# Instance norm over 512 channels: from 32 units of 4 MB in six slots to 23 units of 4 or 6 MB in four slots

## The chip, the cores and the metric

One Trainium2 chip, one of its cores. A core has TensorE (PE), VectorE (DVE), ScalarE (ACT), GpSimd (POOL) and SyncE (SP), a local memory of 128 partitions, a small accumulation memory that TensorE writes (PSUM), and 16 DMA engines that carry data between the chip's main memory and the local one. The metric is the device time of one execution in microseconds (us), lower is better. The kernel before takes 626.87 us (median of 3 runs, 626.81 to 627.3).

## What is computed

```python
def setup_inputs():
    B, G, C_per_g, H, W = 4, 8, 16, 256, 256
    return {
        "x": np.random.randn(B, G, C_per_g, H, W).astype(np.float32),
        "gamma": np.random.randn(G, C_per_g).astype(np.float32),
    }

def reference(x, gamma):
    mu = x.mean(axis=(3, 4), keepdims=True)
    var = ((x - mu) ** 2).mean(axis=(3, 4), keepdims=True)
    x_norm = (x - mu) / np.sqrt(var + 1e-5)
    return (x_norm * gamma[None, :, :, None, None]).astype(np.float32)
```

There are 4 x 8 x 16 = 512 channels of 65,536 float32 values each, 134.2 MB in and 134.2 MB out. Each channel gets its own mean and variance, and one of 128 gammas. A channel must be seen whole before any of it can be written.

## The kernel before

The channels are taken in order, 16 at a time, as 32 *units* of 4 MB (4.194 million bytes). Eight partitions hold one channel, so a unit fills 128 partitions with 8192 values, a row of 32 KB that is contiguous in main memory. Six tiles of 128 x 8192, the *slots* `xt0` to `xt5`, are used in turn.

At the start (L53 to L57) GpSimd issues two small transfers: `touch`, which writes 512 bytes into each of 16 rows of the output (unit 0's store overwrites them), and gamma into one partition (`g_row`). Then the first six units are loaded: units 1 and 3 on ACT's DMA queue, the others on SP's. GpSimd builds `navg` (L63 to L73), a 128 x 128 block matrix with -1/65536 wherever two partitions belong to the same channel. When gamma has landed, one VectorE copy (L80) repeats each gamma eight times, eight small matmuls (L85) turn it into columns, and one copy (L91) stores them as `g_col`. This stands ahead of unit 0 on VectorE.

The loop over units (L104 to L141) is written out in the order in which each engine works:

- VectorE sums the row (L106) into `st`; beside it, ScalarE squares the row and sums the squares (L107). The squares themselves go to `junk` and are not used.
- TensorE multiplies `navg` by the two columns of `st` (L115): every partition then has minus the mean and minus the mean square of its channel in PSUM tile `ps`.
- VectorE makes minus the variance (L116), ScalarE takes the root (L120), VectorE the reciprocal (L124) and the product with gamma (L126), `scale`.
- VectorE writes (x - mean) * scale in place (L135). For unit 0 alone, ScalarE does the last 3/8 of the row (L131, L132).
- The store is issued on ACT's queue (L139), where it waits for VectorE; the next unit's squares stand behind it.
- The load of the unit six ahead is issued on SP's queue (L141, in `load`, L48). It waits until the store of the unit that had the slot is done.

So SP's queue carries loads, ACT's queue carries the stores and two loads, and GpSimd's queue carries only the two small transfers at the start. Order on each engine is program order.

Of the kernel before, what the change touches and what calls it, by code (L numbers as in the profile page):

```python
# [1 line left out]

# [4 lines left out]

F32 = mybir.dt.float32
U8 = mybir.dt.uint8
ALU = mybir.AluOpType  # L10
ACTF = mybir.ActivationFunctionType
AX = mybir.AxisListType


@with_exitstack
def kernel(
    ctx: ExitStack,
    tc: tile.TileContext,
    x: bass.AP,
    gamma: bass.AP,  # L20
    out: bass.AP,
):
    nc = tc.nc
    B, G, C, H, W = x.shape
    P = nc.NUM_PARTITIONS
    HW = H * W
    n_ch = B * G * C
    S = 8
    K = P // S
    F = HW // S  # L30
    U = n_ch // K
    NG = (G * C) // K
    AHEAD = 6
    assert HW % S == 0 and (G * C) % K == 0

    xv = x.rearrange("b g c h w -> (b g c h w)").rearrange("(u p f) -> u p f", p=P, f=F)
    ov = out.rearrange("b g c h w -> (b g c h w)").rearrange("(u p f) -> u p f", p=P, f=F)
    gv = gamma.rearrange("g c -> (g c)")

    data = ctx.enter_context(tc.tile_pool(name="data", bufs=1))  # L40
    singles = ctx.enter_context(tc.tile_pool(name="singles", bufs=1))
    psum = ctx.enter_context(tc.tile_pool(name="psum", bufs=4, space=bass.MemoryType.PSUM))
    ctx.enter_context(tc.manual_schedule())

    slots = [data.tile([P, F], F32, name=f"xt{i}") for i in range(AHEAD)]

    def load(u, queue):
        queue.dma_start(out=slots[u % AHEAD][:], in_=xv[u])  # L48


    g_row = singles.tile([1, G * C], F32, name="g_row")
    touch = singles.tile([16, 128], F32, name="touch")
    nc.vector.memset(touch[:], 0.0)  # L53
    nc.gpsimd.dma_start(out=ov[0][0::S, 0:128], in_=touch[:])  # L54
    nc.gpsimd.dma_start(out=g_row[:], in_=gv[None, :])  # L55
    for u in range(AHEAD):
        load(u, nc.scalar if u in (1, 3) else nc.sync)  # L57

    eps_t = singles.tile([P, 1], F32, name="eps_t")
    nc.gpsimd.memset(eps_t[:], 1e-5)  # L60
    one = singles.tile([1, 1], F32, name="one")
    nc.gpsimd.memset(one[:], 1.0)
    navg = singles.tile([P, K, S], F32, name="navg")  # L63
    nc.gpsimd.memset(navg[:], -1.0 / HW)  # L64
    nc.gpsimd.affine_select(  # L65
        out=navg[:], in_=navg[:], pattern=[[-S, K], [0, S]], compare_op=ALU.is_ge,
        fill=0.0, base=0, channel_multiplier=1,
    )
    nc.gpsimd.affine_select(  # L69
        out=navg[:], in_=navg[:], pattern=[[S, K], [0, S]], compare_op=ALU.is_ge,  # L70
        fill=0.0, base=S - 1, channel_multiplier=-1,
    )
    navg_w = navg[:].rearrange("p k s -> p (k s)")  # L73
    root_eps = singles.tile([P, 1], F32, name="root_eps")
    nc.scalar.activation(out=root_eps[:], in_=eps_t[:], func=ACTF.Sqrt)  # L75
    g_rep = singles.tile([1, NG, K, S], F32, name="g_rep")
    g_ps = psum.tile([P, NG], F32, name="g_ps", bufs=1)
    g_col = singles.tile([P, NG], F32, name="g_col")

    nc.vector.tensor_copy(  # L80
        out=g_rep[:],
        in_=g_row[:].rearrange("o (n k) -> o n k", n=NG).unsqueeze(3).to_broadcast([1, NG, K, S]),
    )
    for n in range(NG):
        nc.tensor.matmul(  # L85
            out=g_ps[:, n : n + 1],
            lhsT=g_rep[:, n].rearrange("o k s -> o (k s)"),
            rhs=one[:],
            start=True, stop=True,
        )  # L90
    nc.vector.tensor_copy(out=g_col[:], in_=g_ps[:])  # L91

    junk = singles.tile([P, F], U8, name="junk")

    st = singles.tile([P, U, 2], F32, name="st")
    nvar = singles.tile([P, U], F32, name="nvar")
    std = singles.tile([P, U], F32, name="std")
    rstd = singles.tile([P, U], F32, name="rstd")
    scale = singles.tile([P, U], F32, name="scale")

    shift = singles.tile([P, 1], F32, name="shift")

    squares = []
    for u in range(U):  # L104
        t = slots[u % AHEAD]
        nc.vector.reduce_sum(out=st[:, u, 0:1], in_=t[:], axis=AX.X)  # L106
        square = nc.scalar.activation(  # L107
            out=junk[:], in_=t[:], func=ACTF.Square, accum_out=st[:, u, 1:2],
        )
        if u:  # L110

            tc.declare_no_dep(square.ins, squares[-1].ins, reason="junk, ordered by the root between")
        squares.append(square)
        ps = psum.tile([P, 2], F32, name="ps")
        nc.tensor.matmul(out=ps[:], lhsT=navg_w, rhs=st[:, u], start=True, stop=True)  # L115
        nc.vector.tensor_scalar(  # L116
            out=nvar[:, u : u + 1], in0=ps[:, 0:1], scalar1=ps[:, 0:1],
            scalar2=ps[:, 1:2], op0=ALU.mult, op1=ALU.add,
        )
        nc.scalar.activation(  # L120
            out=std[:, u : u + 1], in_=nvar[:, u : u + 1], func=ACTF.Sqrt,
            bias=eps_t[:], scale=-1.0,
        )
        nc.vector.reciprocal(out=rstd[:, u : u + 1], in_=std[:, u : u + 1])  # L124
        g = u % NG
        nc.vector.tensor_mul(  # L126
            out=scale[:, u : u + 1], in0=rstd[:, u : u + 1], in1=g_col[:, g : g + 1],
        )
        cut = F * 5 // 8 if u == 0 else F
        if cut < F:  # L130
            nc.vector.tensor_mul(out=shift[:], in0=ps[:, 0:1], in1=scale[:, u : u + 1])  # L131
            nc.scalar.activation(  # L132
                out=t[:, cut:], in_=t[:, cut:], func=ACTF.Identity, bias=shift[:], scale=scale[:, u : u + 1],
            )
        nc.vector.tensor_scalar(  # L135
            out=t[:, :cut], in0=t[:, :cut], scalar1=ps[:, 0:1], scalar2=scale[:, u : u + 1],
            op0=ALU.add, op1=ALU.mult,
        )
        nc.scalar.dma_start(out=ov[u], in_=t[:])  # L139
        if u + AHEAD < U:  # L140
            load(u + AHEAD, nc.sync)  # L141


# [1 line left out]
_INS = ['x', 'gamma']  # L145
_OUTS = [((4, 8, 16, 256, 256), 'float32')]


# [23 lines left out]
```

## Time and profile before

| | |
|---|---|
| median of 3 runs | 626.87 us |
| span of the profiled execution | 625.2 us |
| DVE busy | 441.8 us, 71%, 164 instructions |
| ACT busy | 241.8 us, 39%, 99 instructions |
| PE busy | 21.4 us, 3%, 80 records (each matmul here leaves two) |
| bytes moved | 268.46 MB, 429 GB/s over the span |

The span runs from the first to the last instruction of the profiled execution; the run's time is a little longer, because it also has what lies around the span. The groups of instructions read: line, engine, operation, output <- input, shapes, count | busy us, mean ns of one | idle us before them and what ended it.

```profile
L106 DVE TENSOR_REDUCE st<-xt 128x1 f32<-128x8192 f32 x32 | 277.9, 8684 | 102.2 <-DMA xt<-in_x_dram 102.2
L107 ACT ACTIVATE junk<-xt 128x8192 uint8<-128x8192 f32 x32 | 225.0, 7030 | 272.0 <-DMA xt<-in_x_dram 233.8
L135 DVE TENSOR_SCALAR xt<-xt,ps,scale 128x8192 f32<-128x8192 f32 (+1 forms) x32 | 144.0, 4500 | 1.1
L80 DVE COPY g_rep<-g_row 1x1024 f32<-1x1024 f32 x1 | 0.7, 681 | 14.4 <-DMA g_row<-in_gamma_dram 14.4
L85 PE MATMUL g_ps<-one,g_rep 1*128 1x1 f32 x16 | 3.5, 347 | 16.3 <-DVE g_rep L80 16.3
```

The transfers read: output <- input, queue, operation, count, KB of each, median us from issue to landing.

```profile
out_dram<-xt ACTq DMA_DIRECT2D x32, 4096.0 KB, 62.5
xt<-in_x_dram SPq DMA_DIRECT2D x30, 4096.0 KB, 38.5
xt<-in_x_dram ACTq DMA_DIRECT2D x2, 4096.0 KB, 31.7
out_dram<-touch POOLq DMA_DIRECT2D x1, 8.0 KB, 9.3
g_row<-in_gamma_dram POOLq DMA_DIRECT2D x1, 0.5 KB, 13.5
```

Where the chain of waits says "another core or an unknown queue", SP is waiting for a DMA whose issue the chain could not name.

### The profile page before, as it was taken

How to read it: one execution, taken by the hardware profiler on the slowest of the kernel's cores; microseconds unless marked ns; L12 is line 12 of the kernel's file. 1: busy time of each engine (PE TensorE's matmuls, PEld its weight loads, DVE VectorE, ACT ScalarE, POOL GpSimd, SP SyncE). 2: the span in 40 equal slices, each digit the busy share in tenths (PEclk: the TensorE clock that was granted, in tenths of full speed). 3: DMA queues.
4: the chain of work that ended last, by engine and by line, in shares of the span. 5: the costliest groups of instructions: out<-in, count | busy, mean ns of one | idle time of the engine just before them, and what ended most of it. 6: DMA issues, size and time to landing. Idle time of an engine off the chain costs nothing.

```text
span 625.2 us, 635 instructions
## 1 busy us (share of the span) xinstructions
PE 21.4 (3%) x80; PEld 19.5 (3%) x80; DVE 441.8 (71%) x164; ACT 241.8 (39%) x99; POOL 2.4 (0%) x11
## 2 busy tenths in 40 slices
PE   0200000000000000000000000000000000000000
PEld 0200000000000000000000000000000000000000
DVE  0589999998776687666786767867668676687730
ACT  0464444444443244432344423444224442244400
POOL 1000000000000000000000000000000000000000
DMA  8999999999999999999999999999999999999998
GB/s 370 436 407 432 436 436 436 436 436 430 423 436 434 434 428 434 434 436 436 436 436 428 426 436 436 432 430 434 434 436 436 436 436 421 432 436 434 434 430 367
DMA packets 9282, 268.46 MB, mean 429 GB/s; under 512 B 1072, under 2 KB 1088, under 8 KB 1088
## 3 DMA queue, kind: packets, MB, share of 16 engines
q10 hardware_dynamic: 4896, 142.61, 52.9%
q1 hardware_dynamic: 4320, 125.83, 46.8%
q0 software_dynamic: 64, 0.01, 0.0%
q14 instruction: 2, 0.02, 0.0%
HBM read 134.22 MB, written 134.23 MB: 429 GB/s over the span
## 4 chain that ended last, share of the span: by engine, by line
another core or an unknown queue 61%; DMA 17%; DVE 15%; SPq 1%; PE 1%; issue 0%; ACT 0%
DMA xt<-in_x_dram 10%; DVE st L106 10%; DMA out_dram<-xt 8%; DVE xt L135 5%; SPq L48 1%; PE ps L115 1%; ACT std L120 0%; DVE nvar L116 0%; DVE rstd L124 0%; DVE scale L126 0%; DVE shift L131 0%
## 5 line engine op out<-in xcount | busy, mean ns | idle before, releaser
L106 DVE TENSOR_REDUCE st<-xt 128x1 f32<-128x8192 f32 x32 | 277.9, 8684 | 102.2 <-DMA xt<-in_x_dram 102.2
L107 ACT ACTIVATE junk<-xt 128x8192 uint8<-128x8192 f32 x32 | 225.0, 7030 | 272.0 <-DMA xt<-in_x_dram 233.8
L135 DVE TENSOR_SCALAR xt<-xt,ps,scale 128x8192 f32<-128x8192 f32 (+1 forms) x32 | 144.0, 4500 | 1.1
L120 ACT ACTIVATE std<-nvar,eps_t 128x1 f32<-128x1 f32 x32 | 9.4, 295 | 79.4 <-DVE nvar L116 79.4
L115 PE MATMUL ps<-st,navg 128*128 128x2 f32 x64 | 17.8, 348 | 557.3 <-DVE st L106 557.3
L115 PEld LDWEIGHTS ps<-st,navg 128*128 128x128 f32 x64 | 16.0, 310 | 559.1 <-issue 546.2
L116 DVE TENSOR_SCALAR nvar<-ps 128x1 f32<-128x1 f32 x32 | 9.2, 286 | 23.8 <-PE ps L115 23.8
L124 DVE RECIPROCAL rstd<-std 128x1 f32<-128x1 f32 x32 | 5.2, 163 | 11.6 <-ACT std L120 11.6
L80 DVE COPY g_rep<-g_row 1x1024 f32<-1x1024 f32 x1 | 0.7, 681 | 14.4 <-DMA g_row<-in_gamma_dram 14.4
L107 ACT ACTIVATION_READ_ACCUMULATOR junk<-xt 128x1 f32 x32 | 6.0, 186 | 0.0
L126 DVE TENSOR_TENSOR scale<-rstd,g_col 128x1 f32<-128x1 f32 x32 | 5.1, 158 | 1.1
L85 PE MATMUL g_ps<-one,g_rep 1*128 1x1 f32 x16 | 3.5, 347 | 16.3 <-DVE g_rep L80 16.3
L85 PEld LDWEIGHTS g_ps<-one,g_rep 1*128 1x128 f32 x16 | 3.5, 326 | 16.3 <-issue 16.3
L132 ACT ACTIVATE xt<-xt,shift,scale 128x3072 f32<-128x3072 f32 x1 | 2.9, 2947 | 0.7 <-DVE shift L131 0.7
L91 DVE COPY g_col<-g_ps 128x8 f32<-128x8 f32 x1 | 0.2, 167 | 3.7 <-PE g_ps L85 3.7
L75 ACT ACT_TABLE_LOAD x1 | 1.3, 1283 | 1.7 <-PEq L156 1.7
L53 DVE MEMSET touch<- 16x128 f32 x1 | 0.2, 165 | 0.9 <-PEq L156 0.9
L54 POOL DMA_DIRECT2D out_dram<-touch x1 | 0.6, 617 | 0.8 <-DVE touch L53 0.8
L55 POOL DMA_DIRECT2D g_row<-in_gamma_dram x1 | 0.5, 487 | 0.0
L65 POOL TENSOR_SCALAR_AFFINE_SELECT navg<-navg 128x128 f32<-128x128 f32 x1 | 0.4, 400 | 0.1
L69 POOL TENSOR_SCALAR_AFFINE_SELECT navg<-navg 128x128 f32<-128x128 f32 x1 | 0.4, 399 | 0.1
L64 POOL MEMSET navg<- 128x128 f32 x1 | 0.2, 230 | 0.0
(8 smaller groups left out, 1.0 us busy)
## 6 DMA issues: line engine op xcount, KB each, us to landing
out_dram<-xt ACTq DMA_DIRECT2D x32, 4096.0 KB, 62.5
xt<-in_x_dram SPq DMA_DIRECT2D x30, 4096.0 KB, 38.5
xt<-in_x_dram ACTq DMA_DIRECT2D x2, 4096.0 KB, 31.7
out_dram<-touch POOLq DMA_DIRECT2D x1, 8.0 KB, 9.3
g_row<-in_gamma_dram POOLq DMA_DIRECT2D x1, 0.5 KB, 13.5
```

What stands on the lines that cost most here:

```text
L48: queue.dma_start(out=slots[u % AHEAD][:], in_=xv[u])
L75: nc.scalar.activation(out=root_eps[:], in_=eps_t[:], func=ACTF.Sqrt)
L85: nc.tensor.matmul(out=g_ps[:, n : n + 1], lhsT=g_rep[:, n].rearrange("o k s -> o (k s)"), rhs=one[:], start=True, stop=True,)
L106: nc.vector.reduce_sum(out=st[:, u, 0:1], in_=t[:], axis=AX.X)
L107: square = nc.scalar.activation(out=junk[:], in_=t[:], func=ACTF.Square, accum_out=st[:, u, 1:2],)
L115: nc.tensor.matmul(out=ps[:], lhsT=navg_w, rhs=st[:, u], start=True, stop=True)
L116: nc.vector.tensor_scalar(out=nvar[:, u : u + 1], in0=ps[:, 0:1], scalar1=ps[:, 0:1], scalar2=ps[:, 1:2], op0=ALU.mult, op1=ALU.add,)
L120: nc.scalar.activation(out=std[:, u : u + 1], in_=nvar[:, u : u + 1], func=ACTF.Sqrt, bias=eps_t[:], scale=-1.0,)
L124: nc.vector.reciprocal(out=rstd[:, u : u + 1], in_=std[:, u : u + 1])
L126: nc.vector.tensor_mul(out=scale[:, u : u + 1], in0=rstd[:, u : u + 1], in1=g_col[:, g : g + 1],)
L132: nc.scalar.activation(out=t[:, cut:], in_=t[:, cut:], func=ACTF.Identity, bias=shift[:], scale=scale[:, u : u + 1],)
L135: nc.vector.tensor_scalar(out=t[:, :cut], in0=t[:, :cut], scalar1=ps[:, 0:1], scalar2=scale[:, u : u + 1], op0=ALU.add, op1=ALU.mult,)
```

## The change

There are now 23 units: three of 16 channels, eighteen of 24 channels, two of 16. A unit of 24 channels is 6 MB (6.291 million bytes), 128 rows of 48 KB. A channel is 16 pieces of 4096 values and a row holds three pieces, so a channel takes 5 1/3 rows, and the pieces of one row can belong to two channels. The slots are four tiles of 128 x 12288. All loads are on SP's queue (`split` is empty).

Because of the pieces, a 6 MB unit is computed piecewise: one VectorE sum gives three columns, ScalarE squares three pieces one after another, three matmuls with `navg3` add the pieces up into 24 rows of PSUM (one per channel), the small steps run on 24 partitions with one added copy of the mean, and three further matmuls with `spread` bring each channel's mean and scale back to the 128 partitions, for each piece its own. VectorE then scales the three pieces, with both factors read from PSUM (`wide`). Units of 4 MB are computed as before. At the start, GpSimd builds `navg3` and `spread` besides the old matrix, and gamma is turned into columns by 21 small matmuls (five groups of 16 channels, sixteen groups of 24) with seven small copies.

```diff
-    S = 8
-    K = P // S
-    F = HW // S
-    U = n_ch // K
-    AHEAD = 6
+    F = 4096
+    SLOTS = 4
+    sizes = [2] * 3 + [3] * ((n_ch - 16 * 5) // 24) + [2] * 2
+    U = len(sizes)
+    starts = [sum(sizes[:i]) for i in range(U)]
+    split = {}
+    helped = (0,)
...
-    slots = [data.tile([P, F], F32, name=f"xt{i}") for i in range(AHEAD)]
-    def load(u, queue):
-        queue.dma_start(out=slots[u % AHEAD][:], in_=xv[u])
+    slots = [data.tile([P, 3 * F], F32, name=f"xt{i}") for i in range(SLOTS)]
+    def home(u):
+        return slots[u % SLOTS][:, : sizes[u] * F]
+    def load(u):
+        cut = split.get(u, 0) * F
+        if cut:
+            nc.scalar.dma_start(out=home(u)[:, :cut], in_=rows(xf, u)[:, :cut])
+        if cut < sizes[u] * F:
+            nc.sync.dma_start(out=home(u)[:, cut:], in_=rows(xf, u)[:, cut:])
...
-    for u in range(AHEAD):
-        load(u, nc.scalar if u in (1, 3) else nc.sync)
+    for u in range(SLOTS):
+        load(u)
...
+    for n, c in enumerate(sixteens):
+        nc.vector.tensor_copy(
+            out=g_rep[:, n], in_=g_row[:, c : c + 16].unsqueeze(2).to_broadcast([1, 16, 8]),
+        )
         nc.tensor.matmul(
+            out=g_ps[:, n : n + 1], lhsT=g_rep[:, n].rearrange("o k s -> o (k s)"), rhs=one[:],
             start=True, stop=True,
         )
     nc.vector.tensor_copy(out=g_col[:], in_=g_ps[:])
+    for n, c in enumerate(firsts):
+        nc.tensor.matmul(
+            out=g_ps3[:, n : n + 1], lhsT=g_two[:, c : c + K], rhs=one[:],
+            start=True, stop=True,
+        )
+    nc.vector.tensor_copy(out=g_col3[:], in_=g_ps3[:])
...
+        if three:
+            nc.vector.reduce_sum(
+                out=st[:, u, :, 0], in_=t.rearrange("p (j f) -> p j f", j=3), axis=AX.X,
+            )
+        step = F if three else cols
+        for j in range(cols // step):
+            square = nc.scalar.activation(
+                out=junk[:, :step], in_=t[:, j * step : (j + 1) * step],
+                func=ACTF.Square, accum_out=st[:, u, j, 1:2],
+            )
...
+        if three:
+            for j in range(3):
+                nc.tensor.matmul(
+                    out=ps[:n], lhsT=navg3[:, j], rhs=st[:, u, j], start=j == 0, stop=j == 2,
+                )
...
+        if three:
+            nc.vector.tensor_copy(out=coef[:n, u, 0:1], in_=ps[:n, 0:1])
...
+            for j in range(3):
+                nc.tensor.matmul(
+                    out=wide[:, j], lhsT=spread[:, j], rhs=coef[:n, u], start=True, stop=True,
+                )
+            for j in range(mine):
+                nc.vector.tensor_scalar(
+                    out=t[:, j * F : (j + 1) * F], in0=t[:, j * F : (j + 1) * F],
+                    scalar1=wide[:, j, 0:1], scalar2=wide[:, j, 1:2], op0=ALU.add, op1=ALU.mult,
+                )
...
-        nc.scalar.dma_start(out=ov[u], in_=t[:])
-        if u + AHEAD < U:
-            load(u + AHEAD, nc.sync)
+        nc.scalar.dma_start(out=rows(of, u), in_=t)
+        if u + SLOTS < U:
+            load(u + SLOTS)
```

## The prediction

> **What bounds the kernel now.** I read the slices of the span first, then the chain of waits, then one unit in the timeline, then short windows at the joints.
>
> The slices: is one resource busy all the time?
>
> ```profile
> DMA  8999999999999999999999999999999999999998
> GB/s 370 436 407 432 436 436 436 436 436 430 423 436 434 434 428 434 434 436 436 436 436 428 426 436 436 432 430 434 434 436 436 436 436 421 432 436 434 434 430 367
> ```
>
> The 16 DMA engines are busy in every slice. Only the first, the third and the last fall clearly short. VectorE, the busiest compute engine, stands at 71%.
>
> The chain of waits, in order of time (start, us, what), two units from the middle and one 19 units on:
>
> ```profile
> 160.27 18.95 another core or an unknown queue
> 179.22 0.02 SPq L48
> 179.24 0.03 issue
> 179.27 0.33 SPq L48
> 179.60 18.97 another core or an unknown queue
> ...
> 528.03 18.97 another core or an unknown queue
> ```
>
> SP does nothing but wait until a store has freed a slot, then issues the next load. The beat is (528.03 - 160.27) / 19 = 19.356 us per unit of 8.389 MB (4.194 MB in, 4.194 out): 433.4 GB/s. 32 units at that beat are 619.4 of the 625.2 us. The other 5.8 us are start, end and a break near 40 us.
>
> One unit in the timeline, near the end:
>
> ```profile
> 575.05 0.56 PE L115 MATMUL ps<-st,navg 128*128 128x2 f32 x2 [18.82 <-DVE st L106]
> 576.69 4.55 DVE L135 TENSOR_SCALAR xt<-xt,ps,scale 128x8192 f32<-128x8192 f32 x1
> 581.27 0.34 ACTq L139 DMA_DIRECT2D out_dram<-xt  x1
> 585.57 8.69 DVE L106 TENSOR_REDUCE st<-xt 128x1 f32<-128x8192 f32 x1 [4.33 <-DMA xt<-in_x_dram]
> 600.62 0.34 ACTq L139 DMA_DIRECT2D out_dram<-xt  x1
> ```
>
> A unit takes 600.62 - 585.57 = 15.05 us from landing to its store's issue, so VectorE idles 4.33 us per beat. It is cover, not the bound. The last store is issued 24.6 us before the end although alone it needs 4.194 MB / 433.4 = 9.7 us: older stores are still ahead of it.
>
> Windows at the break and at the end (columns: stretch, length, busy of the five engines, clock, DMA share, GB/s):
>
> ```profile
> 37.00:40.00 3.00, 0.00 (x0) 0.00 (x0) 3.00 (x1) 3.00 (x1) 0.00 (x0) 1.00 0.92 382
> 40.00:43.00 3.00, 0.00 (x0) 0.00 (x0) 3.00 (x1) 3.00 (x1) 0.00 (x0) 1.00 0.97 317
> ...
> 590.00:600.00 10.00, 0.56 (x2) 0.50 (x2) 8.82 (x5) 2.98 (x3) 0.00 (x0) 1.00 1.00 433
> 623.00:625.20 2.20, 0.00 (x0) 0.00 (x0) 0.00 (x0) 0.00 (x0) 0.00 (x0) 1.00 0.00 0
> ```
>
> The break comes when store 0 (issued at 36.48) starts among loads: slice 3 at 407 instead of 436 is (29/436) x 15.63 = 1.0 us. From 590 on only stores of one queue run, still at 433, so one queue alone fills the engines. The last 2.2 us move nothing.
>
> **The change, part by part.** The bytes are the same (268.4 MB), so the floor of 268.4 / 433.4 = 619.4 us stays unless the rate changes. What can move: the rate, the start, a hole in the middle, the end.
>
> *Rate.* 64 transfers of x and out become 46, and rows per DMA engine fall from 64 x 8 = 512 to 80 (ten transfers of 32 KB rows) + 288 (36 of 48 KB) = 368: both 28% fewer. The trace has no 48 KB row, so the saving is bounded. Below: nothing, if the beat is set by bytes alone. Above: the best slices show 436 GB/s, where a beat would be 19.24 us; 0.116 us per unit over 32 units is 3.7 us of overhead, and 28% of it 1.0 us. The beat lies far nearer to the byte time than to any visible row cost, so I take the middle, -0.5 us.
> The Trainium skill ("DMA: Bandwidth & Descriptors", "Where 436 GB/s comes from") gives a ceiling of 435.2 GB/s, and under "Why small descriptors are slow" a fixed cost of some 3 cycles per packet. By that the overhead would be 19.356 - 19.275 = 0.08 us per unit, 2.6 us in all, and the estimated gain 0.7 us. The trace agrees with the ceiling (433 measured); no run here shows how the rest splits.
>
> *A unit on VectorE.* The 6 MB unit: reduce 8.68 x 1.5 = 13.03; three matmuls with the sums, 0.14 + 0.57 + 2 x 0.44 = 1.6 (two records of 0.22 each in the gamma matmuls); variance 0.32, root 0.33 (the new copy of the mean, about 0.17, runs beside it), reciprocal and product 0.4; the three spreading matmuls, 1.6 again; three scalings of 4096 at 2.28 + 0.06 = 7.0. Sum 24.3 us. ScalarE's squares are 3 x (3.5 + 0.2 to 0.3), about 11.3, under the reduce. The DMA time of such a unit is 1.5 x 19.356 = 29.03 us. So the added PE, copy and start costs (+24.3 - 1.5 x 15.05 = +1.7 per unit) are hidden by 4.7 us of idle VectorE, and cost nothing until that is used up. Below (all lost) each would cost 18 x 1.7 = 31 us only if VectorE became the bound.
>
> *Slots.* Four slots hold the same 24 MB. One is at most in computation, so three are loading, stored or waiting; while one queue has rows the engines are full (window 590:600). Waits of SP for a slot stay waits of SP: behind it stand only later loads. On ACT, the store's issue waits for the scaling as now, with the next squares behind it.
>
> *Start.* Loads ahead: 3 x 4.19 + 6.29 = 18.9 MB instead of 25.2, all on SP. Reading the first windows as 433.4 GB/s from about 2.0 us, they would run out at 45.5 us. The first store must come before. Unit 0 lands at about 13 instead of 22.77 (no second queue beside it), but gamma's setup stands first on VectorE: gamma landed 13.5 us after issue with two load queues beside it; with one I take 10 to 12, upper bound 15.5. After it come 21 matmuls at 0.44 = 9.3 and 1 us of copies: unit 0 starts at 20 to 26 and its store goes out 36.48 - 22.77 = 13.7 later, 34 to 39.5. The break of 1.0 us stays. From there store 0 and load 3 share the engines row by row; with store 0 out at 34 both finish near 52 to 55, store 1 is out at 34 + 14.9 = 49, and there is no hole. At 39.5 store 1 comes at 54.4 + 1.2 against 55.2: a hole of 0.4 us at most. Value 0, bounds 0 to +0.4.
>
> *End.* While loads 21 and 22 (16 rows of 32 KB per engine) land, 16 store rows of 48 KB alternate with them. Followed forward from the start by rows, 5.5 store rows of unit 20 are then left: 5.5 x 16 x 49152 B / 433.4 = 10.0 us; store 21 adds 9.7. Store 22 needs 1.3 (completion of its load, my estimate inside the 2.2 us of the last window) + 15.05 + 1.2 (issue to first bytes, 0.81 to 2.0 at the start) = 17.5 us. 19.7 - 17.5 = 2.2 us of cover, where the kernel before had about 13 (24.6 us, less 1.3 to 2.2 us of end, less 9.7). Value 0, thin.
>
> Sum against the profiled 625.2: -0.5 + 0 + 0 + 0 = 624.7. The median of the runs is 1.67 above the profiled span (626.87); I keep that: **626.4 us**.
>
> **Rivals.**
>
> *The break at 40 us goes too (faster).* For it: store 0 now enters an idle queue, not one that has just moved two loads. Against: both windows lie where stores first appear, which happens in either kernel. Price -1.0: 625.4 us, with the larger rate gain 624.9.
>
> *The cover of four slots is too thin at the end (slower).* Place: store 21 ends before store 22 is queued. It decides from 2.2 us of delay of load 22 on, then costs 1 us per us. For it: 32 KB load rows alternate with 48 KB store rows, so the last loads get 40% of the engines, and the last unit then waits for its load alone. Against: my rows say it just fits. If loads got a third, loads 21 and 22 would take 2 x 29.0 instead of 48.4 us: 9.6 late, 7.4 uncovered, 633.8; 3 us late gives 627.2, and with 1 us of hole at the start 628.2.
>
> *48 KB rows cost more than 32 KB rows (slower).* If each is cut in three and each piece bears a row's full share (at most 3.7 us / 512), rows become 80 + 864 = 944: +3.1 us, 630.0. Against: nothing in the trace but the smooth 32 KB rows.
>
> *VectorE becomes the bound (slower).* It needs 4.7 us more per unit. If the 4096-wide scalings ran at the reduce's pace (1.06 ns per element) they would cost 13.0 instead of 7.0: 30.3 us per unit, 1.3 over 29.03, 18 x 1.3 = +23: 650. Against: the same operation at 8192 already takes its first scalar from the same kind of tile.
>
> **How the numbers follow.** Forecast 0.47, its own range 625.8 to 627.0; the break gone 0.23; slower 0.30 (end or start 0.15, rows 0.11, VectorE 0.04). Two runs differ by about 0.2% (1.25 us) without a change, so below 625.6 is faster and above 628.1 slower: 0.23, 0.47, 0.30. The range reaches from the faster rival to the row rival, 625.0 to 630.0, leaving out the dear ends.
>
> **What would show it.** Right: middle slices at 432 to 437 GB/s, loads on a beat of 28.9 to 29.03 us, VectorE idle 4 to 5 us per 6 MB unit, waiting on the load; unit 0's reduce between 20 and 26; no slice under 400 but the ends. Wrong: a DMA share under 0.95 between the last load and the last store (end), near 50 to 57 us (start); a beat over 29.1 with VectorE idle (rows); VectorE without idle time (scaling).

## The result, and the profile after

The changed kernel takes 630.24 us (median of 7 runs, 629.58 to 636.15); the kernel before, on the same chip, 626.87 (7 runs, 626.67 to 627.49). The ratio is 1.0062, 95% interval 1.004 to 1.0085: slower, by 3.4 us or 0.6%. The forecast was 626.4, and 630.0 the end of its range. The profiled execution takes 630.09 with a span of 628.2, 3.0 us more than the span before. (Ratios here leave out runs more than 1.5% above a kernel's fastest; medians and extremes have all runs.)

The slices of the span after:

```profile
DMA  9999999999999999999999999999999999999997
GB/s 368 434 417 423 399 443 434 426 435 438 429 435 437 429 435 438 429 432 441 429 432 441 429 429 438 435 429 438 435 429 438 435 429 438 431 429 438 434 431 309
```

Two things differ from before: the fifth slice (63 to 79 us) is a new one at 399, and the last has 309 instead of 367. The break near 40 us is spread over two slices (417 and 423, where the kernel before has 407 and 432). The middle still averages some 434.

The chain of waits (start, us, what), with the beat of the loads:

```profile
28.70 29.26 DMA out_dram<-xt
...
58.03 31.24 DMA xt<-in_x_dram
89.27 0.02 issue
89.30 12.97 DVE st L161
...
218.83 43.49 DMA xt<-in_x_dram
...
276.82 43.49 DMA xt<-in_x_dram
...
392.79 43.49 DMA xt<-in_x_dram
```

From 218.83 to 392.79 are six 6 MB units: 28.99 us each, 19.33 per 4 MB (19.356 before). Ahead of it stands a stretch that the forecast did not have: from 28.70 to 58.03 the chain waits for store 0 to free its slot, and only then is load 4 issued.

The timeline at the start and at the end:

```profile
10.69 0.21 DVE L119 COPY g_two<-g_row 1x128 f32<-1x128 f32 x1 [9.64 <-DMA g_row<-in_gamma_dram]
13.45 1.44 PE L138 MATMUL g_ps<-one,g_two 1*24 1x1 f32 x32
15.02 8.66 DVE L165 TENSOR_REDUCE st<-xt 128x1 f32<-128x8192 f32 x1
28.70 0.39 ACTq L237 DMA_DIRECT2D out_dram<-xt  x1
43.45 0.34 ACTq L237 DMA_DIRECT2D out_dram<-xt  x1
58.03 0.33 SPq L66 DMA_DIRECT2D xt<-in_x_dram  x1
58.37 0.34 ACTq L237 DMA_DIRECT2D out_dram<-xt  x1
...
552.29 12.95 DVE L161 TENSOR_REDUCE st<-xt 128x3 f32<-128x12288 f32 x1 [5.86 <-DMA xt<-in_x_dram]
568.36 7.09 DVE L221 TENSOR_SCALAR xt<-xt,wide 128x4096 f32<-128x4096 f32 x3 [1.59 <-PE wide L208]
575.48 0.34 ACTq L237 DMA_DIRECT2D out_dram<-xt  x1
591.50 0.34 ACTq L237 DMA_DIRECT2D out_dram<-xt  x1
600.62 8.69 DVE L165 TENSOR_REDUCE st<-xt 128x1 f32<-128x8192 f32 x1 [9.15 <-DMA xt<-in_x_dram]
615.67 0.34 ACTq L237 DMA_DIRECT2D out_dram<-xt  x1
```

Unit 0 starts at 15.02 and store 0 goes out at 28.70; loads 0 to 3 were gone by 57.4, so SP's queue had nothing in it when load 4 was issued. A 6 MB unit takes 575.48 - 552.29 = 23.2 us, with 5.86 us of idle VectorE ahead of it.

To see where the 3 us are, I added up the DMA rows of the two traces themselves. Each DMA engine carries 8 rows of every transfer, one after the other: a 32 KB row takes 1.21 us, a 48 KB row 1.81. (The trace gives a row's queue, start and length, but not its engine. Rows are joined into 16 chains by putting each behind the row that ends where it starts, with 8 rows to a transfer; where several engines wait at once, a row could also belong to another of them.) "Lost" is the time, as a mean over the 16 engines, that is missing against 433.3 GB/s; the last column is the end of the last row.

```
lost, us    0-4   4-60  60-72  72-590  590-end    sum   last row
before     2.64   0.89   0.01    0.27     0.62   4.42     623.93
after      2.71   0.87   1.76   -0.34     2.31   7.31     626.83
```

So: +1.75 just after load 4 was issued, -0.6 from the beat, +1.7 at the end, in sum +2.9. The break near 40 us is worth what it was (0.87 against 0.89 from 4 to 60). The two losses belong together in this execution, as the rows of single engines show. "Spread" is how far apart the first and the last of the 16 engines finish a transfer:

```
loads finished near, us     31-41   56-61   87-81   142-139   200-197   548-545
spread before, us             0.5     0.5     0.5       0.5       1.0       1.0
spread after, us              0.6     1.0     2.4       3.0       4.3       4.3
```

(The two times of a column are after and before.) Load 4 met engines 1.0 us apart, nearly a row. Rows then took up to 1.58 us longer than their size asks, beginning with rows of store 1 at 60.9, ahead of load 4's first row at 62.5. About 1.4 of the 1.76 us are slow rows and 0.4 are eight short gaps between rows. The engines left the place 3 us apart. From then on every unit waits for the latest engine, while the early ones run ahead. At the end that can't be hidden: load 22 is on the first engine at 595.9 and on the last at 600.2, so its unit starts at 600.62, and its store's first rows run at 616.5. Fifteen engines had finished store 21 at 613.6 to 616.1 and stood idle; the latest finished it at 617.1, went straight on, and ended last, at 626.8. The window (columns: stretch, length, busy of the five engines, clock, DMA share, GB/s) has the idle engines:

```profile
612.00:616.00 4.00, 0.00 (x0) 0.00 (x0) 3.64 (x1) 0.00 (x0) 0.00 (x0) 1.00 0.61 262
```

### The profile page after: what moved, and what is told of

Its sections match the earlier page's. It is cut to its first block, busy times and chain, and to the rows that moved or that the text cites. A ratio compares the mean times of both kernels' runs of the same rounds, so it can differ in the third digit from the quotient of the medians.

```text
span 628.2 us, 1055 instructions
## 1 busy us (share of the span) xinstructions
PE 38.4 (6%) x268; PEld 36.0 (6%) x268; DVE 441.0 (70%) x180; ACT 247.1 (39%) x144; POOL 4.4 (1%) x17
## 4 chain that ended last, share of the span: by engine, by line
DMA 73%; DVE 21%; PE 2%; ACT 1%; issue 1%; POOL 0%; SPq 0%; ACTq 0%
DMA xt<-in_x_dram 52%; DMA out_dram<-xt 20%; DVE st L161 14%; DVE st L165 3%; DVE xt L221 2%; DMA g_row<-in_gamma_dram 1%; DVE xt L233 1%; ACT xt L229 0%; PE wide L208 0%; ACT std L191 0%; PE ps L179 0%; DVE nvar L187 0%; PE g_ps L129 0%; DVE rstd L197 0%; PE g_ps L138 0%
## 5 line engine op out<-in xcount | busy, mean ns | idle before, releaser
L168 ACT ACTIVATE junk<-xt 128x4096 uint8<-128x4096 f32 (+1 forms) x59 | 230.4, 3906 | 301.1 <-DMA xt<-in_x_dram 288.7
L161 DVE TENSOR_REDUCE st<-xt 128x3 f32<-128x12288 f32 x18 | 233.2, 12953 | 100.4 <-DMA xt<-in_x_dram 100.4
L221 DVE TENSOR_SCALAR xt<-xt,wide 128x4096 f32<-128x4096 f32 x54 | 127.6, 2420 | 28.6 <-PE wide L208 28.6
L165 DVE TENSOR_REDUCE st<-xt 128x1 f32<-128x8192 f32 x5 | 43.4, 8679 | 10.2 <-DMA xt<-in_x_dram 10.2
L191 ACT ACTIVATE std<-nvar,eps_t 24x1 f32<-24x1 f32 (+1 forms) x23 | 6.8, 293 | 60.5 <-DVE nvar L187 60.5
L208 PE MATMUL wide<-coef,spread 24*128 24x2 f32 x108 | 25.4, 347 | 20.7 <-DVE coef L204 20.7
L208 PEld LDWEIGHTS wide<-coef,spread 24*128 24x128 f32 x108 | 24.3, 321 | 21.7 <-issue 20.6
L233 DVE TENSOR_SCALAR xt<-xt,ps,coef 128x8192 f32<-128x8192 f32 (+1 forms) x5 | 21.1, 4229 | 0.1
L183 PE MATMUL ps<-st,navg 128*128 128x2 f32 x10 | 2.8, 348 | 76.7 <-DVE st L165 76.7
L183 PEld LDWEIGHTS ps<-st,navg 128*128 128x128 f32 x10 | 2.5, 310 | 77.0 <-issue 64.1
```

The lines of the kernel that those rows point to most:

```text
L161: nc.vector.reduce_sum(out=st[:, u, :, 0], in_=t.rearrange("p (j f) -> p j f", j=3), axis=AX.X,)
L165: nc.vector.reduce_sum(out=st[:, u, 0, 0:1], in_=t, axis=AX.X)
L168: square = nc.scalar.activation(out=junk[:, :step], in_=t[:, j * step : (j + 1) * step], func=ACTF.Square, accum_out=st[:, u, j, 1:2],)
L183: nc.tensor.matmul(out=ps[:], lhsT=navg2[:].rearrange("p k s -> p (k s)"), rhs=st[:, u, 0], start=True, stop=True,)
L191: nc.scalar.activation(out=std[:n, u : u + 1], in_=nvar[:n, u : u + 1], func=ACTF.Sqrt, bias=eps_t[:n], scale=-1.0,)
L208: nc.tensor.matmul(out=wide[:, j], lhsT=spread[:, j], rhs=coef[:n, u], start=True, stop=True,)
```

## The experiments

Kernels are the one before ("before") or the changed one ("changed") with the edit shown. Each was run beside the kernel before on the same chip, whose median was 626.9 to 627.1 every time.

### All loads on SP, in the kernel before

```diff
-        load(u, nc.scalar if u in (1, 3) else nc.sync)
+        load(u, nc.sync)
```

> The kernel before, with all six loads ahead on SP's queue. Theory R (restart: what costs time is the load queue running empty while stores run, and starting again): six loads are queued before the first store's completion is needed, so the queue never empties; same time as before within 0.1% (626.3 to 627.5). Theory S (one load queue at the start is itself the loss): slower by 2 to 3 us. Theory W (48 KB rows are the loss): same time.

629.74 us (10 runs, 627.1 to 636.06), ratio 1.0049 [1.0028, 1.0071]. One line of the change alone costs 2.8 us. There is no stall here: lost from 60 to 72 us is 0.05. But when store 0 ended, 13 engines had carried 32 load rows (four loads, exactly) and three had carried 33. Twelve of the thirteen end at 622.98 to 623.46; the three, and one that fell off later, at 624.3, 625.4, 626.3 and 627.15. From 60 to 590 us the three lose 2.2 to 3.5 us each, in 24 to 27 slow rows at the ends of transfers. Theories R and W, which expected no change (the queue never runs empty, and there are no 48 KB rows), fall for this kernel; the size is what theory S said.

### Five slots, in the kernel before

```diff
-    AHEAD = 6
+    AHEAD = 5
```

> The kernel before with five slots instead of six; rows stay 32 KB. Load 5 now has to wait for store 0, while load 4 and store 0 end together near 61 us, so the load queue is empty for some 2 us and restarts among stores. Theory R: a second stall of 1 to 3 us just after 62 us, DMA rate under 380 GB/s there, and the DMA engines end a transfer 2 us or more apart from then on; 628 to 630 us. Theory W: no stall, 626.5 to 627.5. Theory E (too little cover at the end): the cover shrinks from about 13 to about 11 us, so no change.

629.01 us (12 runs, 628.16 to 636.65), 1.0042 [1.0021, 1.0063]. The load queue runs empty and load 5, issued at 62.4, restarts it: 0.25 us are lost at 64 to 68 and 0.68 at 76 to 80, and the spread of the stores goes from 0.4 to 3.6. One engine took a row of load 5 a turn before the others did, and ends last. The other 15 were 0.4 us apart when store 0 ended and took load 5's first row at the same turn, and yet each has slow rows there. So a queue that runs empty and restarts costs time without 48 KB rows, new arithmetic or a new start order.

### No 4 MB units at the start, in the changed kernel

```diff
-    sizes = [2] * 3 + [3] * ((n_ch - 16 * 5) // 24) + [2] * 2
+    sizes = [3] * ((n_ch - 16 * 2) // 24) + [2] * 2
```

> The changed kernel with all units but the last two of 6 MB (20 of 24 channels, 2 of 16): 25.2 MB are loaded ahead instead of 18.9, store 0 is done before the loads ahead are, and the load queue never empties. Theory R: no second stall near 60 us, about 2 us less than the changed kernel or more: 626 to 628 us. Theory W: 630 us as the changed kernel. Theory E (end): 630 us, since the last two units are the same.

630.03 us (6 runs, 628.62 to 632.4), 1.0051 [1.0036, 1.0066]. Load 4 is issued at 73.66, while load 3 runs until 79.9: the queue never runs empty. Nothing is lost at 60 to 72 (0.02 us gained). The stall has gone; the time hasn't. When store 0 ended, three engines had carried 29 load rows and thirteen 30, and the spread of the loads grows from 2.6 to 4.5; but only one of the three ends late (625.18, in the profiled run of 628.62, the fastest). The stall is not the only way to lose step, and theory R alone falls.

### More instructions, in the kernel before

```diff
         nc.tensor.matmul(out=ps[:], lhsT=navg_w, rhs=st[:, u], start=True, stop=True)
+        for _ in range(7):
+            nc.tensor.matmul(out=dump[:], lhsT=navg_w, rhs=st[:, u], start=True, stop=True)
```

> The kernel before with seven more matmuls per unit into a tile that nobody reads (about 450 more TensorE records; the result is not touched). The trace of the changed kernel has two instruction transfers of 16 KB near 193 and 544 us on a DMA engine, each putting that engine behind by 1 us or more; the kernel before has none until its end. Theory I (the longer program): instruction transfers appear in the middle of the span and the time rises by 0.5 to 1.5 us. Theory R alone: no change in time, 626.3 to 627.5.

628.02 us (11 runs, 627.71 to 628.17), 1.0015 [1.0006, 1.0024]. `dump` is used by nobody, and its 14 records per unit (0.35 us each, 3.1 us together since they overlap) run on an otherwise idle TensorE, behind the one product that VectorE waits for. The page's list of DMA queues (packets, MB, share) has a queue that the kernel before lacks:

```profile
q8 instruction: 4, 0.07, 0.0%
```

and in the changed kernel:

```profile
q8 instruction: 2, 0.03, 0.0%
```

Each is one transfer of 16 KB that a single DMA engine carries between its rows, 0.88 to 0.96 us. In this experiment the spread jumps from 0.6 to 2.1 us at the first. A longer program costs DMA time, on one engine at a time, and the engine isn't given less to do for it. The kernel with four is 1.1 us slower, as theory I said. In the profiled run an engine without such a transfer ended at 625.01, as late as the latest one with (625.06), so they need not be all of it.

### Two queues at the start, in the changed kernel

```diff
-    split = {}
+    split = {1: 2, 3: 3}
```

> The changed kernel with loads 1 and 3 on ACT's queue again, as before. Theory S (one load queue at the start is the loss): back to 627 to 627.6 (before, less 0.7 for fewer rows, plus about 1 for instruction transfers). Theory J (join: what costs time is a queue that ran empty and joins again while the other queue runs; it stalls the DMA engines and leaves some of them behind for good): four slots still leave SP's queue empty from about 46 us until store 0 is done, so a join remains: 628.5 to 631, with a wide spread of runs.

627.69 us (11 runs, 627.11 to 631.4), 1.002 [1.0008, 1.0032]. Loads 1 and 3 go on ACT's queue, as in the kernel before; 2.5 of the 3.4 us are gone; this is close to what theory S gave (627 to 627.6), and J falls. The rows of 48 KB and the last two units are those of the changed kernel, so neither of them is the loss of these 2.5 us. A window of ten microseconds in the kernel before, in the changed kernel, then here; a row counts where it starts, so such a window is right to a few per cent:

```profile
60.00:70.00 10.00, 0.48 (x2) 0.39 (x2) 9.05 (x5) 3.77 (x2) 0.00 (x0) 1.00 1.02 439
```

```profile
60.00:70.00 10.00, 0.00 (x0) 0.00 (x0) 10.00 (x1) 9.89 (x6) 0.00 (x0) 1.00 1.02 382
```

```profile
60.00:70.00 10.00, 0.29 (x2) 0.20 (x1) 9.24 (x5) 3.96 (x3) 0.00 (x0) 1.00 1.03 446
```

Load 4 is issued at 57.58, as late as in the changed kernel, into an empty queue again. What differs is the state in which it meets the engines. Here are rows of four engines in each (start, L for a row of a load, A for one of a store, + the ns beyond what its size takes):

```
changed
61.96A+664  65.67L+251  67.73A      68.94L
62.00A+741  64.45L+1122 67.38A      68.59L
61.58A+387  63.18L+1583 66.58A      67.79L
61.33A+420  62.96L+470  65.24A      66.45L+305
two queues at the start
61.49L      63.31A      64.52L      66.33A
61.57L      63.38A      64.59L      66.40A
61.65L      63.46A      64.67L      66.48A
61.98L      63.80A      65.01L      66.82A
```

In the changed kernel's first two lines the engine stands idle between the first row and the second. With two queues all 16 engines take the first row of load 4 at the same turn, after four rows of store 1, 0.5 us apart, and no row is slow. In the changed kernel 14 engines take it after five rows of store 1 and two after four. So two things differ at once: how far apart the engines are, and at which row of the store the load comes.

### One load on ACT, in the kernel before

```diff
-        load(u, nc.scalar if u in (1, 3) else nc.sync)
+        load(u, nc.scalar if u == 1 else nc.sync)
```

> The kernel before with load 3 moved from ACT's queue to SP's; load 1 stays on ACT's. Loads 0 and 1 still run side by side to 22 us, the first store is issued at the same time, but it now enters an empty queue in the middle of a load instead of following load 3. Theory S: as before, 626.3 to 627.5, since the start still has two queues. Theory J: one join, 628 to 630.5, and some DMA engines end 1 us or more after the others.

627.06 us (11 runs, 626.96 to 627.43), 1.0000 [0.9991, 1.0009]. Store 0 enters an empty queue in the middle of load 3, all engines at load row 30, and nothing is lost, as theory S said; J falls. That a queue joins need not cost anything.

### A load held back in mid-span, in the kernel before

```diff
+        if u == 16:
+            continue
+        if u == 17:
+            for p in (0, 16):
+                nc.sync.dma_start(out=slots[17 % AHEAD][p : p + 16, 0:16], in_=xv[23][p : p + 16, 0:16])
+            load(22, nc.sync)
```

> The kernel before with load 22 held back once, in the middle of the span, until store 17 is done instead of store 16 (two transfers of 1 KB into store 17's slot stand ahead of it on SP's queue; the next load overwrites them). SP's queue runs empty once for about 1 to 2 us and joins again; the start, the slots and the rows are those of the kernel before and stores keep the engines busy. Theory J: +1 to +3 us and a wider spread of runs, with the DMA engines further apart after that point. Theory S, or any theory in which only the start counts: 626.3 to 627.5.

634.84 us (12 runs, 628.42 to 644.9), 1.0055 [1.0026, 1.0084] over seven of them. The two small SP transfers hold load 22 until store 17 is done; SP's queue runs empty at 391.7 and load 22 is issued at 393.73. The small transfers' rows of 64 bytes come first, one in each turn of the loads, so load 22's first rows run from 400.2 on: the edit adds these turns to the restart. Together they cost 1.4 to 10.7 us in the seven runs, different each time; the other five lie higher, and no trace shows why. In the profiled run (628.47) three engines have 169 load rows behind them when store 19 ends and the others 168, and the spread of the stores goes from 1.2 to 2.4 at once and to 3.1 later. Theories in which only the start counts fall.

### The first store a little later, in the kernel before with all loads on SP

```diff
+        if u == 0:
+            nc.vector.reduce_sum(out=late[:], in_=t[:, :320], axis=AX.X)
```

and the same with 700 and with 1088 columns: an unused sum ahead of unit 0's was to delay store 0 by 0.4, 0.8 and 1.2 us. In the profiles it was issued 0.52, 0.83 and 1.09 us later than in the first experiment (28.86).

> e1 (the kernel before, all loads on SP's queue) with the first store 0.4 us later, by one short sum on VectorE whose result nobody reads. In e1's trace the first store's rows reach the DMA engines between 31.5 and 32.1 us, while 16 engines end a row one after another; three engines take the store one row of 1.21 us later than the others, and these three end the span late. Theory K (out of step: a queue that joins costs time when its join falls between the row ends of the engines, because some engines then serve it a row later and stay behind, losing more at each transfer; a join that meets all engines in the same row is harmless): the join moves by a third of a row; 627 if it is clear of the row ends, 628 to 631 if not. Theory S (a start on one queue is itself the loss): 629.7 as e1.

> The same with the first store 0.8 us later, two thirds of a row. Theory K: the engines' row ends spread over 0.7 us of a row of 1.21 us, so at least one of e8 and this run should be clear of them: 626.6 to 627.4 with a narrow spread of runs, and in its trace all 16 engines serve the first store after the same number of load rows. Theory S: 629.7.

> The same with the first store 1.2 us later, one whole row, so that the join should meet the engines as it did in e1. Theory K: 628.5 to 631 again, with one to some engines a row off. Theory S: 629.7.

```
store 0 meant later, us  0 (first experiment)    0.4      0.8      1.2
median, us                  629.74             636.62   645.94   644.17
ratio                       1.0049             1.0141   1.0296   1.0271
load rows at store 0's end  13x32, 3x33        9x32, 7x33  16x33   16x33
```

(4 runs each; intervals 1.0113 to 1.017, 1.0279 to 1.0313, 1.0254 to 1.0288.) I expected the split among the engines to be what costs, so that all of them in one step would be well. The opposite came out, and both theories fall: with all 16 at row 33 the spread is 0.7 us at store 0's end, and it grows to 13.4 by the end. The slices of the 700-column kernel:

```profile
GB/s 379 436 401 438 423 423 428 428 428 424 419 430 423 417 428 411 428 430 411 430 409 428 438 419 425 421 425 432 425 421 415 430 419 425 425 425 413 430 336 281
```

No slice is bad; nearly all are a little low, down to 336 and 281 where the early engines have finished. The slow rows stand where transfers end: from 60 to 590 us, 153 first rows of a load are slow by 0.6 us on average (1.35 at most), the next two by 0.2. Set beside the others: an engine on which stores end one row behind loads (33 = 4 x 8 + 1; 169 = 21 x 8 + 1) loses at the ends of transfers, in all five kernels that had such engines (this series, all loads on SP, the held load). Engines on which they end together (32), or 4 to 6 rows apart (28, 30, 36, 37), mostly do not; but in the 320-column kernel eight of the nine engines at 32 lose 6.3 to 8.3 us from 60 to 590, no less than the seven at 33 (2.4 to 7.1). So the one row is a sign that goes with the loss, not a cause that these runs isolate.

### The first store later, in the changed kernel

```diff
+            if u == 0:
+                nc.vector.reduce_sum(out=late[:], in_=t[:, :700], axis=AX.X)
```

and with 7000 columns, which puts store 0 at 36.06 us, where two queues at the start had put it.

> The changed kernel with its first store 0.8 us later. There the first store meets all engines in the same row, but the restart of the loads near 60 us finds row ends spread over 1.2 us and scatters the engines. Theory K: the restart moves with store 0, but the spread is as long as a row, so it should hardly matter when it comes: 629 to 631. If the spread shrinks by chance, down to 627.7 (e5). Theory S: 630.2.

> The changed kernel, loads on SP's queue alone, with its first store 7.4 us later (a sum of 7000 columns on VectorE whose result nobody reads), so that the stores start where they do in e5, near 36 us. Theory S (the single load queue at the start is the loss): 629.5 to 630.5 as the changed kernel. Theory T (when the first store and the restart of the loads near 60 us fall relative to the rows under way is the loss; which queue carries the loads ahead is not): the restart is met by engines in step or not, so clearly different from 630.2; 627.2 to 628 as e5 if in step, over 632 if a store's end falls one row behind a load's.

700 columns: 629.52 us (4 runs), 1.0042 [1.0027, 1.0057], and the stall stays: 1.91 us lost at 60 to 72, the time that theories K and S expected. 7000 columns: 628.96 us (12 runs, 627.08 to 636.07), 1.0038 [1.0017, 1.006], and there is no stall; the window of the 7000-column kernel reads as with two queues:

```profile
60.00:70.00 10.00, 0.07 (x1) 0.00 (x0) 9.45 (x5) 4.14 (x4) 0.00 (x0) 1.00 1.03 446
```

So in these kernels the stall hangs on the moment at which store 0 and load 4 come, not on which queue the loads are on. But the stall's going brings 627.1 only in the best runs. In the profiled one (631.91) a single engine drifts away without any one bad place: the spread of the loads goes from 0.4 to 6.7 us, and 5.7 us are lost after 590. Neither S nor T gave 628.96.

### One load on ACT, and the third store later, in the changed kernel

```diff
-    split = {}
+    split = {1: 2}
```

```diff
+            if u == 2:
+                nc.vector.reduce_sum(out=late[:], in_=t[:, :4000], axis=AX.X)
```

> The changed kernel with load 1 alone on ACT's queue; loads 0, 2 and 3 on SP's. Theory S: 627.2 to 628 as e5, since loads 0 and 1 start side by side. Theory T: nothing general; the first store comes near 36 us as in e5, but enters an empty queue in the middle of load 3.

> The changed kernel with store 2 4.2 us later. In its trace load 4 (issued at 58.03) and store 2 (issued at 58.37) are issued 0.3 us apart, just before the stall of 60 to 67 us; in e5, which has no such stall, they are 8 us apart (57.6 and 66.0). Theory N (neighbours: two issues at once make the stall): no stall near 60 us and 628 to 628.8. Theories S and T: the restart is met by the same engines in the same rows, so the stall stays: 629.5 to 631.

One load on ACT: 629.91 us (9 runs, 627.73 to 631.28), 1.0037 [1.0024, 1.005]. No stall (0.04 us lost at 60 to 72), yet no gain: one engine was a row off at 62.8 (36 load rows against 37), and the spread grows from 2.1 to 7.4. A second engine, in the same rows as the other 14, falls 5.8 us behind and ends last. Theory S falls: that two loads start side by side is not enough. Third store later: 630.15 us (6 runs, 628.83 to 632.41), 1.0055 [1.0041, 1.0069]. In the changed kernel store 2 was issued 0.34 us after load 4; moving it away changes nothing, 1.91 us are lost as before:

```profile
60.00:70.00 10.00, 0.00 (x0) 0.00 (x0) 10.00 (x2) 6.95 (x3) 0.00 (x0) 1.00 1.01 356
```

That the two issues hinder each other (theory N) falls. No version tried beats the kernel before: 627.06 with one load on ACT is equal to it, 627.69 is the best with 6 MB units.

## Why the prediction was wrong, point by point

*Rate: right.* Taken: -0.5, between 0 and -1.0. Measured: 19.356 - 19.33 = 0.026 us per 4 MB, 0.8 us over 32; the rows give 0.6 from 72 to 590 us. The estimate of 0.7 from the Trainium skill ("DMA: Bandwidth & Descriptors", "Why small descriptors are slow") agrees in size; no run here separates the cost of a row from the rest.

*A unit on VectorE: right.* 23.1 to 23.2 us against 24.3 worked out, under a beat of 28.99. The difference is the matmuls with 24 columns, 0.37 us for six records where I took 1.6 from rows of 128 columns. VectorE waits 5.86 us per unit for its load, so neither it nor the 48 KB rows (1.81 us, 1.5 times 1.21) became the bound; both of these rivals fall.

*Start: this step failed.* It is where the loads ahead run out and SP's queue restarts. It was valued at 0, with "there is no hole", on the ground that "one queue alone fills the engines". In the step itself three things were off. Unit 0 was to start at 20 to 26 and started at 15.02 (gamma landed 8.7 us after its issue, not 10 to 12, and 32 gamma records took 1.4 us, not the 7 that go into 9.3); store 0 was to go out at 34 to 39.5 and went out at 28.70; and I asked only whether a store's rows were there when load 3 and store 0 ended together, not whether a load's were, though just 18.9 MB of loads are issued ahead. Loads 0 to 3 and store 0 ended together at 57 us, and load 4 could be issued only then; that is so with store 0 out at 36 too (load 4 at 57.25 with 7000 columns, 57.58 with two queues), so it lay inside the forecast's own case. There is nearly no hole in the sense of an empty engine (0.4 us): store 1's rows were there. What the row-by-row reckoning left out is that the restart of a queue can itself cost: 1.75 us, mostly slow rows, and engines 3 us apart. Two of the signs named in advance show it: a slice under 400 that is not an end (399), and idle engines between the last load and the last store (a share of 0.61 from 612 to 616). The third, a share under 0.95 near 50 to 57 us, does not: slow rows count as busy (1.02 from 60 to 70).

That the restart can cost, and need not, is shown: nothing is lost there with two queues or 7000 columns, 1.8 to 1.9 us in the changed kernel, with 700 columns and with the third store later. What decides it is not shown. Where nothing was lost, the engines were 0.3 to 0.5 us apart and took the load after four rows of the store; where much was, they were 0.8 to 1.0 apart and most took it after five. Five slots had engines 0.4 apart, 15 of them after five rows, and lost 0.25 and 0.68 us: being close together is not enough by itself. Nor does the stall account for all of the time: without it one load on ACT still takes 629.91 and 7000 columns 628.96.

*All loads on SP, costed at nothing: wrong as well.* In the kernel before it costs 2.8 us alone. The Trainium skill has my premise ("DMA: Bandwidth & Descriptors", "Issuing engines are not separate DMA queues"): transfers of all issuing engines run on the same 16 engines and interleave. The rows agree that they do, one of a load after one of a store; it doesn't follow that it is the same where they are put, 1.0049 [1.0028, 1.0071].

*Instruction transfers: left out.* The program grew from 80 to 268 TensorE records, and two 16 KB transfers came into the span, at 193.5 and 543.9 us. The first falls on the engine that ends last, and the spread goes from 3.3 to 4.3: about 1 us. I had counted the new instructions as hidden under VectorE's idle time, which holds on the engines that run them.

*End: right term, wrong size.* The cover of 2.2 us, called thin, was reckoned for engines in step. Load 22 spread over 4.3 us, and 1.7 us more than before were lost after 590. The rival "The cover of four slots is too thin at the end" came true in that sense, though not by the share between loads and stores that I gave it: the slots would have been enough for engines in step. That last clause is argued from the cover; no run here tries it.

*The other rivals.* The break at 40 us did not go (0.87 us lost from 4 to 60, 0.89 before).

*Sum.* -0.6 (rate), +1.75 (restart), +1.7 (end, from the restart's spread and the instruction transfer) and 0.07 at the very start give 2.9; the span is 3.0 longer.

What stays open: what makes rows slow at a restart, and whether the engines' distance or the row of the store decides it; why kernels whose stores end one row behind loads are dear; and why in some runs single engines drift without any such place (7000 columns, one load on ACT). The runs of most of these kernels lie 3.6 to 9 us apart, those of the kernel before within 1.1.

## What to carry to other kernels

Where the DMA engines are busy from end to end, a mean rate isn't enough: what counts is the latest of the 16, so look at how far apart they finish one transfer, above all after a queue ran empty and was refilled. Before depth is traded for size, follow the loads as well as the stores to the moment when the first slot comes free, and judge a change in start order by several runs, since one profile shows one of many outcomes: the runs of the 7000-column kernel lie 9 us apart. Count a longer program as traffic on the same engines.

## What the runs showed of the hardware

- Each DMA engine carries 8 of the 128 rows of each transfer and is given no less when it is late. In the changed kernel what the latest engine had lost by 200 us (spread 4.3) it still lacked at 600 (4.3).
- With rows in both queues an engine takes one row of each in turn, 48 KB against 32 KB too: 61.49 L, 63.31 A, 64.52 L, 66.33 A; even a row of 64 bytes takes a turn (held load).
- A 0.8 us later first store made one kernel 16 us slower (629.74 to 645.94), with no compute engine more than 1 us busier (VectorE 442.1 and 442.9).
- A program of 528 TensorE records drew four 16 KB instruction transfers through the data path, one of 268 drew two; 0.88 to 0.96 us each, on one engine.
